# Attention outputs: reciprocals of the softmax sums spread by GpSimd's DMAs through DRAM, outputs multiplied and split by GpSimd, low part of q by VectorE

## The chip, the cores and the metric

The kernel runs on one core of one Trainium2 chip. The metric is the device time of one execution in microseconds, as a median of three runs. The core has five engines, each working through its own list of instructions in order: PE (TensorE, with its weight loads shown apart as PEld), DVE (VectorE), ACT (ScalarE), POOL (GpSimd) and SP (SyncE, which issues most DMAs). Some DMAs are issued from POOL.

## The reference

One layer of a diffusion backbone over 1024 latent tokens and 256 context tokens, in fp32. What matters here is the attention between the two feed-forward halves, and that its output is projected afterwards.

```python
def gqa_attend(q, k, v):
    s = jnp.einsum('btkgd,blkd->bkgtl', q, k, preferred_element_type=jnp.float32) * (HEAD_DIM ** -0.5)
    p = jax.nn.softmax(s, axis=-1).astype(v.dtype)
    return jnp.einsum('bkgtl,blkd->btkgd', p, v)
...
        x = x + 0.5 * ml[2] * swiglu(modulate(rms_norm(x, norm1_g[layer]), ml[0], ml[1]),
                                      ffn1_w_in[layer], ffn1_w_out[layer])
...
        o_l = latent_attention(q_l, k_all, v_all)

        x = x + ml[5] * merge_branches(y_conv_l, o_l, gt_l, w_branch_conv[layer],
                                       w_branch_attn[layer], w_out[layer])
...
        x = x + 0.5 * ml[8] * swiglu(modulate(rms_norm(x, norm3_g[layer]), ml[6], ml[7]),
                                      ffn2_w_in[layer], ffn2_w_out[layer])
    return rms_norm(x, final_g)
```

There are 8 query heads on 2 key heads, each 128 wide; 1024 latent queries look at 1280 keys.

## The kernel before

**Precision.** Every fp32 product is three matmuls (`mm3`): each operand is split into a high part, rounded to the fast matmul type, and a low part, what is left; high by high, high by low and low by high are added up in PSUM. A split is therefore two instructions: a copy that rounds (on ACT, a CAST in the profile) and a subtraction (on DVE unless told otherwise).

**Attention.** The work is cut into 16 units: 8 heads, each with the queries 0 to 511 (`C0`) and 512 to 1023 (`C1`). Unit 0 is head 0 with `C0`, unit 15 is head 7 with `C1`. A unit goes through these steps:
- `begin`: q of the unit is split into the two `qs` tiles of 128x512; the high part by ACT, the low part by POOL.
- `scores`, four times, for 128 queries each: matmuls against the context keys (`kc`) and twice 512 latent keys (`kl`); DVE finds the maxima (`m`, `nm`), ACT takes the exponentials (`pc`, `pl`) and sums each row on the way, DVE adds the sums (`rsum`).
- `turn`, ten times, one for each 128 keys: PE transposes four 128x128 blocks into a PSUM bank (`pt`), and the bank is split into `pts`, high part by ACT, low part by DVE. There are two such banks.
- `values`, ten times: three matmuls of `pts` with the values add up in the one PSUM bank `po`. Turns run three steps ahead of values (`AHEAD = 3`).
- `output`: four rows of sums become reciprocals (`rinv`, 128 queries on the partitions by 4), PE transposes each, spread over 128 columns, into a `pt` bank, so that each partition holds the 512 reciprocals; ACT copies `po` to the head's tile `q` of 128x1024, and DVE multiplies the copy by the bank.

**What runs beside it.** The loop over `units[1:]` writes the scores of a unit between the turns and values of the unit before it. Up to unit 12 or so it also has `fillers`: matmuls of the convolution branch, which give PE something else to do. They run out at about 1740 us, and what follows, from there to about 1867 us, is called the tail here: scores of the last units, turns and values, and after the last scores turns and values alone. At the end of the tail come the merges (projections of the head outputs), which need all heads' outputs in split form: `split_output` makes `oh` and `ol` of 128x1024 for each head. From unit 13 on the loop writes the splits of heads 0 to 5 between the steps; head 6 follows, then head 7 in two halves of 512.

**Order.** The kernel is written in the Tile framework; a scheduler settles each engine's order when the program is built, so instructions move ahead of the place where they are written if their operands allow it. In this way parts of the later stage `late_steps` come into the tail: tiles of 128x512 of the modulation weights are loaded (`rawm`, by SP), and DVE adds them up (`macc`).

**Tiles that are shared.** `ttile` hands out 11 buffers of 128x512: `qs`, `rawm`, and the loads `ga` and `z` of the merges take turns in them. SP issues loads in order, so a load that waits for a buffer holds back the loads behind it. The heads' outputs and the `pl` and `pc` tiles are among 38 buffers of 128x1024. All instructions go through the helper `Engine.issue`, so the profile calls all of them line 90; they are told apart by their tiles.

Of the kernel before, what the change touches and what calls it, by code (L numbers as in the profile page):

```python
# [9 lines left out]
F32 = mybir.dt.float32  # L10
# [8 lines left out]
P = 128  # L19
# [7 lines left out]
NQ = 8  # L27
# [8 lines left out]
C0, C1, CC = ("l", 0, 512), ("l", 512, 512), ("c", 0, CT)  # L36
# [15 lines left out]
def tile_dit_layer(  # L52
# [44 lines left out]
    act, dve, pool, pe, sp = (Engine(e) for e in (nc.scalar, nc.vector, nc.gpsimd, nc.tensor, nc.sync))  # L97
# [7 lines left out]
    dram = ctx.enter_context(tc.tile_pool(name="dram", bufs=1, space=DRAM))  # L105
# [3 lines left out]
    def uniq(s):  # L109
        n_tiles[0] += 1  # L110
        return f"{s}_{n_tiles[0]}"

    def atile(name, shape=(P, SLOT), dt=F32):
        return apool.tile(list(shape), dt, tag="A", name=uniq(name))

    def ttile(name, n=512, dt=F32):
        t = tpool.tile([P, 512], dt, tag="t", name=uniq(name))
        return t[:, :n]

    def small(name, n, dt=F32):  # L120
        return spool.tile([P, n], dt, tag=f"s{n}_{name}", name=uniq(name))
# [4 lines left out]
    def ps_t(n=512):  # L126
        return psum.tile([P, 512], F32, tag="t", name=uniq("pt"), bufs=2)[:, :n]
# [4 lines left out]
    def matmul(out, w, x, start, stop, pinned=False, on=False):  # L132

        inst = pe.matmul(out, w, x, start=start, stop=stop, skip_group_check=on)
        if pinned:
            tc.keep_in_program_order(inst)

    def transpose(out, in_, pinned=False):
        n = in_.shape[0]
        inst = pe.transpose(out, in_, ident[:n, :n])  # L140
        if pinned:
            tc.keep_in_program_order(inst)
# [43 lines left out]
    def col(name, k=0):  # L186
        o = voff[name] + k
        return cols[:, o : o + 1]
# [8 lines left out]
    def split(src, hi, lo, lo_eng=None, hi_eng=None):  # L197

        if hi_eng is dve:
            dve.tensor_copy(out=hi, in_=src)  # L200
        else:
            act.copy(out=hi, in_=src)
        (lo_eng or dve).tensor_sub(out=lo, in0=src, in1=hi.bitcast(F32))
# [257 lines left out]
    def run(steps, n=None):  # L461

        if n is None:
            for _ in steps:
                pass
        else:
            for _ in range(n):
                next(steps, None)
# [597 lines left out]
    for k in range(4):  # L1066
        if k % 2:
            half1.shifted(h0[k][:, 0], k, xh[k])
        else:
            dve.tensor_scalar(  # L1070
                out=h0[k][:, 0], in0=xh[k], scalar1=gain1["l"][:, k : k + 1], scalar2=modl[:, k : k + 1],
# [43 lines left out]
    hd = dram.tile([NH, P, L], F32, name="hd")  # L1115
# [85 lines left out]
    for j in range(NH):  # L1201
        half1.side = side(j) if j >= SIDE_FROM else None
        u, c = half1.next_first()
        v, b = half1.second(u)
# [25 lines left out]
    for d in range(0, KD, 2):  # L1230
        t = ttile("cx")
# [7 lines left out]
        for e in range(2):  # L1239
            te = t[:, e * CT : (e + 1) * CT]  # L1240
            dve.scalar_tensor_tensor(
                out=te, in0=pt[:, e * CT : (e + 1) * CT], scalar=gate1["c"][:, d + e : d + e + 1], in1=te, op0=ALU.mult, op1=ALU.add
# [71 lines left out]
    for i in range(KD):  # L1314
        u = atile("u")
# [5 lines left out]
        for ch, bg, gc in mixed():  # L1321
            gate(gcd, i, ch, gc)
            o = ch[1]
            y = ttile("y")
            dve.tensor_scalar(out=y, in0=u[:, o : o + 512], scalar1=col("w1", i), scalar2=None, op0=ALU.mult)
            for j in (0, 2):
                a, b = max(o, 1 - j), min(o + 512, L + 1 - j)
                ya = y[:, a - o : b - o]
                dve.scalar_tensor_tensor(
                    out=ya, in0=u[:, a + j - 1 : b + j - 1], scalar=col(f"w{j}", i), in1=ya, op0=ALU.mult, op1=ALU.add  # L1330
# [42 lines left out]
    for kt in range(10):  # L1373
        ch = CC if kt < 2 else C0 if kt < 6 else C1
        o = (kt if kt < 2 else (kt - 2) % 4) * P
# [67 lines left out]
    q_f = []  # L1443
# [65 lines left out]

    o_parts = [None] * NQ  # L1510

    def split_output(hd, *chunks):
        if o_parts[hd] is None:
            o_parts[hd] = atile("oh", dt=F32R), atile("ol", dt=F32R)
        a, b = chunks[0][1], chunks[-1][1] + 512
        split(q_f[hd][:, a:b], *(t[:, a:b] for t in o_parts[hd]))

    class Unit:
        def __init__(self, hd, ch):
# [2 lines left out]
        def begin(self):  # L1522
            o = self.ch[1]
            self.qs = [ttile("qs", dt=F32R) for _ in range(2)]
            split(q_f[self.hd][:, o : o + 512], *self.qs, pool)
            self.pc = atile("pc", (P, 4, CT))
            self.pl = []
            self.rsum = small("rsum", 4)
# [37 lines left out]
        def values(self, kt, pts):  # L1566
# [5 lines left out]
            matmul(po, vh, pts[:, 1], start=False, stop=False)  # L1572
            matmul(po, vl, pts[:, 0], start=False, stop=(kt == 9))

        def output(self):
            rinv = small("rinv", 4)
            of = q_f[self.hd][:, self.ch[1] : self.ch[1] + 512]
            dve.reciprocal(out=rinv[:], in_=self.rsum[:])
            pr = ps_t()
            for qt in range(4):  # L1580
                transpose(pr[:, qt * P : (qt + 1) * P], rinv[:, qt : qt + 1].to_broadcast([P, P]))
            act.copy(out=of, in_=self.po)
            dve.tensor_mul(out=of, in0=of, in1=pr)

    def seconds():

        turned = []

        def value():
            u, kt, pts = turned.pop(0)  # L1590
            u.values(kt, pts)
            if kt == 9:
                u.output()

        for u in units:
            for kt in range(10):
                turned.append((u, kt, u.turn(kt)))
                if len(turned) > AHEAD:
                    value()
                yield  # L1600
        while turned:
            value()
            yield
# [4 lines left out]
    def merge(j, ch):  # L1608

        if j not in m_hi:  # L1610
            m_hi[j], m_lo[j] = atile("mh", dt=F32R), atile("ml", dt=F32R)
        if j not in wa:
            wa[j] = load_cols(w_ba[0], j * P)
        w, o = wa[j], ch[1]
        ga, z = ttile("ga"), ttile("z")
        sp.dma_start(out=ga, in_=gad[j, :, o : o + 512])
        sp.dma_start(out=z, in_=zd[j, :, o : o + 512])
        ps = ps_s()
        terms = [
            (w[0][:, k], w[1][:, k], *(t[:, o : o + 512] for t in o_parts[k])) for k in range(KD)  # L1620
        ]
        for k in range(KD - 1):
            mm3(ps, terms, k, k + 1)
            yield
        mm3(ps, terms, KD - 1)
        dve.tensor_mul(out=ga, in0=ga, in1=ps)
        dve.tensor_add(out=ga, in0=ga, in1=z)
        split(ga, m_hi[j][:, o : o + 512], m_lo[j][:, o : o + 512])
        yield

    units = [Unit(hd, ch) for hd in range(NQ) for ch in (C0, C1)]
    u = units[0]
# [26 lines left out]
    for n_unit, u in enumerate(units[1:], 1):  # L1659
        u.begin()  # L1660
        for n in (3, 2, 3, 2):
            u.scores(len(u.pl))
            for _ in range(n):
                run(rest, 1)
                if len(u.pl) < 4:
                    run(fill, 1)
            if n == 2:
                run(fill, 1)
            if n == 2 and n_unit >= 13:
                split_output(next(to_split), C0, C1)  # L1670
    run(fill)
    run(rest, 4)
    split_output(NQ - 2, C0, C1)
    split_output(NQ - 1, C0)
    merges = (step for j in range(2) for step in merge(j, C0))
    for _ in rest:
        run(merges, 2)
    run(merges)
    split_output(NQ - 1, C1)


    for j in range(KD):
# [7 lines left out]
    for ch in (C0, C1):  # L1690
        o = ch[1]
        for d in range(KD):
# [7 lines left out]
                out=xs(d, ch), in0=ps, scalar=modl[:, 40 + d : 41 + d], in1=xs(d, ch), op0=ALU.mult, op1=ALU.add  # L1700
# [16 lines left out]
        out=gf[:], in0=cols[:, voff["gf"] : voff["gf"] + 8], scalar1=math.sqrt(D), scalar2=None, op0=ALU.mult  # L1717
# [46 lines left out]
    for j in range(NH):  # L1764
        if j > 1:
            run(last_steps, 3)
        u, c = fast.next_first()
        v, b = fast.second(u)
# [81 lines left out]
```

## Time and profile before

| | us |
|---|---|
| median of three runs | 2693.46 (2692.87 to 2695.69) |
| the profiled execution, its own time | 2692.97 |
| its span, from the first to the last instruction | 2691.1 |
| PE busy in the span | 2646.4 |
| DVE busy | 2016.0 |
| ACT busy | 1178.8 |
| POOL busy | 513.8 |
| attention: copy of the first unit's output, of the last | 1516.34, 1866.86 |

An engine's busy time is summed over its instructions, with overlaps counted once. Idle time of an engine costs something only where another waits for it. The views used below are: the page; the instructions of one tile; busy time in stretches of the span; the timeline of one engine; and the chain of waits, which goes back from the last instruction of a stretch to whatever released each piece of work. In the chain a row has its start, its length, the engine and the tile (or the DMA) that it stands for.

### The profile page before, as it was taken

The numbers are of one execution on the slowest core, as the hardware profiler recorded it, in microseconds if no ns is written. First come the engines' busy times: TensorE is split into PE (matmuls) and PEld (weight loads), VectorE is DVE, ScalarE is ACT, GpSimd is POOL, SyncE is SP. The second block draws the span as 40 slices with busy tenths as digits, with TensorE's granted clock in tenths as the row PEclk, the third lists the DMA queues.
The fourth block names the chain that finished last, engine by engine and source line by source line (L and its number), as shares of the span: only waits on it lengthen the run. The fifth ranks groups of instructions, "written<-read, shape, count | busy, mean of one in ns | idle before, by whom it ended". The sixth has DMA issues, their size and how long they took to land.

```text
span 2691.1 us, 36996 instructions
## 1 busy us (share of the span) xinstructions
PE 2646.4 (98%) x13437; PEld 2228.1 (83%) x13437; DVE 2016.0 (75%) x3363; ACT 1178.8 (44%) x2324; POOL 513.8 (19%) x403
## 2 busy tenths in 40 slices
PE   8999999999999999999999999999999999999998
PEld 5787899888778878888999888877888788888888
DVE  5788966888887899877487666785658886667885
ACT  6523454433454633333245666664236333334453
POOL 0144201221010044333023111000001442321200
PEclk9999999999999999999999999999999999999999
DMA  8565465346974345332213311011733552327841
GB/s 317 196 204 176 146 215 173 117 126 215 286 179 122 111 155 180 108 111 94 80 48 105 112 48 44 28 52 59 246 119 129 180 168 87 95 86 278 192 91 63
DMA packets 368206, 372.68 MB, mean 138 GB/s; under 512 B 18822, under 2 KB 257560, under 8 KB 368024
## 3 DMA queue, kind: packets, MB, share of 16 engines
q1 hardware_dynamic: 359000, 353.03, 39.9%
q0 software_dynamic: 9024, 17.30, 4.0%
q8 instruction: 105, 1.72, 0.3%
q14 instruction: 77, 0.63, 0.1%
HBM read 302.59 MB, written 67.63 MB: 138 GB/s over the span
## 4 chain that ended last, share of the span: by engine, by line
PE 91%; DVE 4%; DMA 2%; issue 2%; ACT 1%; POOL 0%; SPq 0%; DVEq 0%; POOLq 0%; ACTq 0%
PE ps L90 75%; PE pt L90 8%; PE po L90 7%; DMA rawm<-in_w_mod_dram 1%; DVE r L90 1%; DVE macc L90 0%; DMA ws<-in_ffn_w_out_dram 0%; DVE wl L90 0%; DVE nt L90 0%; DMA raw<-in_ffn_w_in_dram 0%; POOL s L90 0%; DVE uc L90 0%; DVE y L90 0%; DVE m L90 0%; DVE ol L90 0%
## 5 line engine op out<-in xcount | busy, mean ns | idle before, releaser
L90 PE MATMUL ps<-r,wl 128*128 128x512 f32 x5196 | 1206.5, 391 | 10.3 <-DVE wl L90 4.2
L90 PEld LDWEIGHTS ps<-r,wl 128*128 128x128 f32 x5196 | 974.1, 189 | 219.3 <-DVE wl L90 6.3
L90 ACT CAST wl<-s 128x512 fp32r<-128x512 f32 x254 | 156.7, 619 | 321.2 <-PE ps L90 218.7
L90 POOL TENSOR_TENSOR s<-raw 128x512 f32<-128x512 f32 x64 | 94.4, 1474 | 1051.2 <-DMA raw<-in_ffn_w_in_dram 630.7
L90 ACT CAST wl<-raw 128x512 fp32r<-128x512 f32 x287 | 177.5, 619 | 215.3 <-PE ps L90 153.9
L90 DVE TENSOR_TENSOR wl<-raw,wl 128x512 fp32r<-128x512 f32 x287 | 201.9, 705 | 62.1 <-ACT wl L90 60.3
L90 DVE TENSOR_TENSOR wl<-s,wl 128x512 fp32r<-128x512 f32 x254 | 230.4, 908 | 19.9 <-ACT wl L90 18.5
L90 POOL TENSOR_TENSOR s<-raw,s 128x512 f32<-128x512 f32 x64 | 103.8, 1623 | 361.1 <-DVE wl L90 361.1
L90 DVE SCALAR_TENSOR_TENSOR macc<-rawm,silu_c,macc 128x512 f32<-128x512 f32 x178 | 148.7, 852 | 25.0 <-DMA rawm<-in_w_mod_dram 24.3
L90 PE MATMUL ps<-wh,r 128*128 128x256 f32 x768 | 141.6, 285 | 0.0
L90 DVE TENSOR_TENSOR pts<-pt,pts 128x512 fp32r<-128x512 f32 x160 | 108.6, 686 | 41.4 <-ACT pts L90 40.2
L90 DVE TENSOR_TENSOR u<-u,ps 128x512 f32<-128x512 f32 x174 | 118.0, 678 | 27.8 <-PE ps L90 27.7
L90 ACT CAST pts<-pt 128x512 fp32r<-128x512 f32 x160 | 92.8, 592 | 89.5 <-PE pt L90 87.9
L90 DVE TENSOR_REDUCE m<-ps 128x1 f32<-128x512 f32 (+1 forms) x192 | 110.9, 595 | 26.0 <-PE ps L90 24.9
L90 ACT CAST rh<-hid 128x512 fp32r<-128x512 f32 x132 | 81.2, 620 | 107.1 <-PE ps L90 90.4
L90 PE MATMUL ps<-rh,wl 128*128 128x512 f32 x360 | 122.4, 390 | 2.8 <-ACT rh L90 2.8
L90 PEld LDWEIGHTS ps<-wh,r 128*128 128x128 f32 x768 | 120.6, 192 | 0.0
L90 PE MATMUL po<-pts,vh 128*128 128x512 f32 x256 | 111.7, 443 | 1.5 <-ACT pts L90 1.4
L90 PE MATMUL ps<-wl,r 128*128 128x256 f32 x384 | 108.8, 283 | 0.0
L90 PE MATMUL ps<-kl,qs 128*128 128x512 f32 x384 | 106.2, 397 | 0.4 <-ACT pc L90 0.4
L90 DVE TENSOR_TENSOR rl<-hid,rh 128x512 fp32r<-128x512 f32 x132 | 89.9, 684 | 21.7 <-PE ps L90 12.0
L90 ACT CAST wh<-raw 128x512 fp32r<-128x512 f32 (+1 forms) x85 | 67.9, 801 | 84.1 <-PE ps L90 57.7
(312 smaller groups left out, 5100.7 us busy)
## 6 DMA issues: line engine op xcount, KB each, us to landing
raw<-in_ffn_w_in_dram SPq DMA_DIRECT2D x130, 512.0 KB
raw<-in_ffn_w_out_dram SPq DMA_DIRECT2D x72, 512.0 KB
rawm<-in_w_mod_dram SPq DMA_DIRECT2D x136, 256.0 KB
raw<-in_w_in_dram SPq DMA_DIRECT2D x61, 512.0 KB
hid<-hd SPq DMA_DIRECT2D x40, 512.0 KB
ws<-in_ffn_w_out_dram POOLq DMA_DIRECT2D x30, 512.0 KB, 6.5
ucd<-uc SPq DMA_DIRECT2D x25, 512.0 KB
hd<-c SPq DMA_DIRECT2D x40, 256.0 KB
```

The lines of the kernel that those rows point to most:

```text
L90: inst = getattr(self.engine, name)(*args, **kw)
```

## The change

`output` loses the transposes. Instead, a new method `inverse`, written after the fifth `values` step of a unit, takes the reciprocals and issues two DMAs from POOL: the first writes the 128x4 reciprocals to a row of 512 numbers in DRAM, in the order of the queries (each element of 4 bytes goes to a place of its own); the second reads that row back to each of the 128 partitions, into a `ttile` called `rrow`. `output` is then ACT's copy of `po` and a multiplication by POOL. The splits of heads 0 to 6 go from ACT and DVE to POOL, both instructions; the two halves of head 7 (`late=True`) stay with ACT and DVE. The low part of `qs` goes from POOL to DVE.

```diff
-    def split_output(hd, *chunks):
+    def split_output(hd, *chunks, late=False):
         if o_parts[hd] is None:
             o_parts[hd] = atile("oh", dt=F32R), atile("ol", dt=F32R)
         a, b = chunks[0][1], chunks[-1][1] + 512
-        split(q_f[hd][:, a:b], *(t[:, a:b] for t in o_parts[hd]))
+        hi, lo = (t[:, a:b] for t in o_parts[hd])
+        if late:
+            split(q_f[hd][:, a:b], hi, lo)
+        else:
+            pool.tensor_copy(out=hi, in_=q_f[hd][:, a:b])
+            pool.tensor_sub(out=lo, in0=q_f[hd][:, a:b], in1=hi.bitcast(F32))
...
-            split(q_f[self.hd][:, o : o + 512], *self.qs, pool)
+            split(q_f[self.hd][:, o : o + 512], *self.qs)
...
+        def inverse(self):
+            rinv = small("rinv", 4)
+            dve.reciprocal(out=rinv[:], in_=self.rsum[:])
+            row = dram.tile([512], F32, name=uniq("rinvd"))
+            pool.dma_start(out=row.rearrange("(j p) -> p j", p=P), in_=rinv[:])
+            self.rows = ttile("rrow")
+            pool.dma_start(out=self.rows, in_=row.partition_broadcast(P))
+
         def output(self):
-            rinv = small("rinv", 4)
             of = q_f[self.hd][:, self.ch[1] : self.ch[1] + 512]
-            dve.reciprocal(out=rinv[:], in_=self.rsum[:])
-            pr = ps_t()
-            for qt in range(4):
-                transpose(pr[:, qt * P : (qt + 1) * P], rinv[:, qt : qt + 1].to_broadcast([P, P]))
             act.copy(out=of, in_=self.po)
-            dve.tensor_mul(out=of, in0=of, in1=pr)
+            pool.tensor_mul(out=of, in0=of, in1=self.rows)
...
             u.values(kt, pts)
+            if kt == 4:
+                u.inverse()
             if kt == 9:
                 u.output()
...
     split_output(NQ - 2, C0, C1)
-    split_output(NQ - 1, C0)
+    split_output(NQ - 1, C0, late=True)
...
-    split_output(NQ - 1, C1)
+    split_output(NQ - 1, C1, late=True)
```

The scheduler settles the order anew. Three places matter below. The first is PE where unit 12 ends and the values of unit 13 (`po_17316` before, `po_17303` after) begin; `rinv_17276` are unit 12's reciprocals, `vc` and `vh` parts of the values. Before:

```order
L90 MATMUL po_17316<-pts_17248,vc_11566 128x512 x3
L90 MATMUL po_17316<-pts_17259,vc_11566 128x512
L90 MATMUL pt_17278<-ident,rinv_17276 128x128 x4
L90 MATMUL po_17316<-pts_17259,vc_11566 128x512 x2
L90 MATMUL po_17316<-pts_17270,vh_11562 128x512
```

and with the change:

```order
L90 MATMUL po_17303<-pts_17242,vc_11566 128x512 x3
L90 MATMUL po_17303<-pts_17253,vc_11566 128x512
L90 MATMUL ps_17549<-kc_11851,qs_17434 128x256 x2
L90 MATMUL ps_17549<-kc_11851,qs_17435 128x256
L90 MATMUL pt_17295<-ident,pl_16994 128x128
L90 MATMUL pt_17295<-ident,pl_17052 128x128
L90 MATMUL pt_17295<-ident,pl_17103 128x128
L90 MATMUL pt_17295<-ident,pl_17165 128x128
L90 MATMUL po_17303<-pts_17253,vc_11566 128x512 x2
L90 MATMUL po_17303<-pts_17264,vh_11562 128x512
```

The four transposes of reciprocals, which took one of the two `pt` banks, are gone; a turn and three of unit 15's score matmuls stand there.

The second is DVE where the first sums of the modulation weights (`macc`) stand. Before, they follow the last row sum and reciprocal, unit 15's, in the stretch of its last scores:

```order
L90 SCALAR_TENSOR_TENSOR macc_3284_17932<-rawm_17978,silu_c,macc_3284_17932 128x512
L90 SCALAR_TENSOR_TENSOR macc_3284_17932<-rawm_17981,silu_c,macc_3284_17932 128x512
L90 TENSOR_REDUCE rsum_17446<-rs_17625 128x1
L90 RECIPROCAL rinv_17888<-rsum_17446 128x4
L90 SCALAR_TENSOR_TENSOR macc_3284_17932<-rawm_17984,silu_c,macc_3284_17932 128x512
L90 TENSOR_TENSOR pts_17136<-pt_17131,pts_17136 128x512
L90 TENSOR_TENSOR pts_17147<-pt_17142,pts_17147 128x512
L90 SCALAR_TENSOR_TENSOR macc_3284_17932<-rawm_17987,silu_c,macc_3284_17932 128x512
L90 TENSOR_TENSOR pts_17158<-pt_17153,pts_17158 128x512
```

With the change they begin later, among the turns of unit 14:

```order
L90 TENSOR_SCALAR macc_3300_17916<-rawm_17917,silu_c 128x512
L90 TENSOR_TENSOR pts_17491<-pt_17486,pts_17491 128x512
L90 TENSOR_TENSOR pts_17527<-pt_17522,pts_17527 128x512
L90 SCALAR_TENSOR_TENSOR macc_3300_17916<-rawm_17920,silu_c,macc_3300_17916 128x512
L90 TENSOR_TENSOR pts_17539<-pt_17534,pts_17539 128x512
L90 SCALAR_TENSOR_TENSOR macc_3300_17916<-rawm_17923,silu_c,macc_3300_17916 128x512
L90 TENSOR_TENSOR pts_17578<-pt_17573,pts_17578 128x512
L90 SCALAR_TENSOR_TENSOR macc_3300_17916<-rawm_17926,silu_c,macc_3300_17916 128x512
L90 TENSOR_TENSOR pts_17589<-pt_17584,pts_17589 128x512
```

The sums have moved past the last scores, and two or three of the turns' subtractions stand between them; `rawm_17923` lies in the buffer that `rrow_17383`, unit 13's, had.

The third is POOL, which before had nothing between its last `qs` and the work of the second feed-forward half. With the change this stands there (`rrow_17156` is unit 12's row, `rrow_17383` unit 13's, `rrow_17610` unit 14's, `rrow_17795` unit 15's; `q_13261` is head 6, `q_13262` head 7):

```order
L90 CAST oh_17545<-q_12921 128x1024
L90 TENSOR_TENSOR q_13261<-q_13261,rrow_17156 128x512
L90 TENSOR_TENSOR ol_17546<-q_12921,oh_17545 128x1024
L90 CAST oh_17657<-q_12922 128x1024
L90 DMA rinvd_17793<-rinv_17791 128x4x1
L90 TENSOR_TENSOR ol_17658<-q_12922,oh_17657 128x1024
L90 DMA rrow_17795<-rinvd_17793 128x512
L90 TENSOR_TENSOR q_13261<-q_13261,rrow_17383 128x512
L90 CAST oh_17708<-q_13261 128x1024
L90 TENSOR_TENSOR ol_17709<-q_13261,oh_17708 128x1024
L90 TENSOR_TENSOR q_13262<-q_13262,rrow_17610 128x512
L90 TENSOR_TENSOR q_13262<-q_13262,rrow_17795 128x512
```

Products of units 12 to 15, splits of heads 4 to 6 and unit 15's two DMAs share one queue, in this order.

## The prediction

> **What bounds the kernel now.** I read the page first, then busy time by stretches around the attention, then the chain of waits in the attention's tail, then single tiles for durations. From the page:
>
> ```profile
> span 2691.1 us, 36996 instructions
> PE 2646.4 (98%) x13437; PEld 2228.1 (83%) x13437; DVE 2016.0 (75%) x3363; ACT 1178.8 (44%) x2324; POOL 513.8 (19%) x403
> ```
>
> ```profile
> PE 91%; DVE 4%; DMA 2%; issue 2%; ACT 1%; POOL 0%; SPq 0%; DVEq 0%; POOLq 0%; ACTq 0%
> ```
>
> PE is busy for 98% of the span and makes 91% of the chain. POOL has 0% of the chain: it is the engine with room. So the change can gain in two ways only: by PE work that goes away, and by stalls of PE that go away. Where the stalls are is seen in busy time by stretches (columns: stretch, its length, then each engine's busy time with instructions, the granted PE clock, DMA share, GB/s):
>
> ```profile
> 1490.00:1740.00 250.00, 248.90 (x1364) 209.07 (x1363) 167.37 (x367) 160.83 (x410) 35.54 (x20) 1.00 0.17 55
> 1740.00:1860.00 120.00, 112.57 (x622) 91.20 (x621) 88.84 (x163) 73.48 (x164) 0.00 (x0) 0.97 0.15 45
> ...
> 1790.00:1815.00 25.00, 21.25 (x106) 16.54 (x105) 18.11 (x34) 14.93 (x34) 0.00 (x0) 0.86 0.21 63
> ...
> 1776.00:1790.00 14.00, 12.98 (x78) 10.70 (x77) 13.00 (x29) 10.14 (x26) 0.00 (x0) 1.00 0.31 95
> 1795.00:1805.00 10.00, 6.52 (x37) 4.70 (x35) 7.64 (x16) 6.22 (x15) 0.00 (x0) 0.90 0.39 113
> 1826.00:1833.00 7.00, 5.76 (x34) 4.49 (x34) 4.22 (x7) 3.10 (x5) 0.00 (x0) 1.00 0.00 0
> ```
>
> While the convolution's matmuls fill in (1490 to 1740), PE is idle for 1.1 of 250 us: there every matmul removed is time saved, and no stall can be. In the tail it is idle for 7.4 of 120 us, and in the 25 us from 1790 its granted clock is 0.86, which makes 21.25 us of matmuls some 0.14 x 21.25 = 3.0 us longer than at full clock. DVE is busy for 13.0 of the 14 us from 1776. What PE waits for there is in the chain of waits of the tail, at two places:
>
> ```profile
> 1796.52 2.76 DMA rawm<-in_w_mod_dram
> 1799.30 0.76 DVE macc L90
> 1800.08 2.68 DMA rawm<-in_w_mod_dram
> 1802.78 0.75 DVE macc L90
> 1803.54 0.61 DVE pts L90
> ...
> 1804.19 1.12 PE pt L90 x4
> ```
>
> ```profile
> 1827.73 0.70 DVE q L90
> 1828.45 1.06 ACT oh L90
> 1829.53 1.22 DVE ol L90
> 1830.75 0.61 DVE pts L90
> ...
> 1831.41 0.66 PE pt L90 x4
> ```
>
> At the first, a sum for a later stage stands in DVE's queue and waits for its load; the subtraction `pts` stands behind it, and PE's next transposes wait for the bank that `pts` would free. At the second, the product, the split of head 6 on ACT and DVE, and again a `pts` behind them.
>
> **The change part by part.** First the transposes of the reciprocals. Their group and what four transposes take in the chain when PE runs undisturbed:
>
> ```profile
> L90 PE MATMUL pt<-ident,rinv x64: 270/272/275, 1518.2 to 1856.5; 128*128 128x128 f32 x64
> ```
>
> ```profile
> 1818.74 0.44 PE pt L90 x4
> 1819.17 0.70 PE po L90 x3
> 1819.88 0.44 PE pt L90 x4
> ```
>
> 272 ns is the modelled length of one, overlapping the next; four advance the chain by 0.44 us. 64 of them are 16 x 0.44 = **7.0 us of PE** gone. Units 0 to 8 end before 1740, so 9 x 0.44 = 4.0 us lie where PE is never idle and are safe; the other 3.1 us lie in the tail, 94% busy, and I count them whole. A turn's bank is also held 16 times less often.
>
> Second, what leaves and joins the other engines, by these rows:
>
> ```profile
> L90 POOL TENSOR_TENSOR qs<-q,qs x16: 1282/1290/2072, 1456.3 to 1709.9; 128x512 fp32r<-128x512 f32 x16
> L90 DVE TENSOR_TENSOR q<-q,pt x16: 676/686/689, 1518.9 to 1867.7; 128x512 f32<-128x512 f32 x16
> L90 ACT CAST oh<-q x9: 614/1047/1072, 1755.3 to 1869.3; 128x1024 fp32r<-128x1024 f32 x7, 128x512 fp32r<-128x512 f32 x2
> L90 DVE TENSOR_TENSOR ol<-q,oh x9: 685/1215/1227, 1756.5 to 1870.2; 128x1024 fp32r<-128x1024 f32 x7, 128x512 fp32r<-128x512 f32 x2
> ```
>
> ```profile
> L90 POOL TENSOR_TENSOR wc<-raw,wc 128x1024 fp32r<-128x1024 f32 x9 | 21.6, 2395 | 110.0 <-ACT wc L90 110.0
> ```
>
> DVE loses 16 products (16 x 0.69 = 11.0) and 7 subtractions (7 x 1.22 = 8.5), and gains 16 subtractions for q's low part, which I take at the same 0.69 (11.0): 8.5 us less, all in the tail. ACT loses 7 x 1.05 = 7.3 us there. POOL gets 16 products at 1.29, 7 subtractions at 2.40, 7 roundings of 128x1024, which no row shows: between 1.2 (half of the two-operand 2.40) and 2.40, I take 1.8; and 32 DMAs. Of those the nearest rows are POOL's own loads for issuing, and for landing the transfer that spreads one row over 128 partitions, from SP's issue at 2304.9 to the DVE instruction that waits for it:
>
> ```profile
> L90 POOL DMA_DIRECT2D ws<-in_ffn_w_out_dram x36: 1199/1222/1444, 701.1 to 2582.6; - x36
> DMA to landing us min/median/max: 5.7/6.5/10.9
> ```
>
> ```profile
> L90 SPq DMA_DIRECT2D mcol<-mrow x1: 476/476/476, 2304.9 to 2304.9; - x1
> ...
> 2307.80 1.10 DVE L90 TENSOR_TENSOR modl<-mcol,bcol 128x4 f32<-128x4 f32 x1 [1.80 <-DMA mcol<-mrow]
> ```
>
> A DMA takes 1.2 us to issue on POOL, up to 2.4 if 512 elements of 4 bytes cost double; it lands after between 2.9 us (2 KB, as here) and 10.9 us (up to 512 KB). I take 1.2 and 2.9, since the sizes are those of `mcol`. POOL waits in its queue for the first landing before it issues the second DMA, and products and splits queue behind that.
>
> Does POOL keep up? The copies of `po`, after which a product can start, come at
>
> ```profile
> 1812.57 0.59 ACT q L90
> ...
> 1825.41 0.59 ACT q L90
> ...
> 1839.45 0.59 ACT q L90
> ```
>
> for units 12, 13 and 14: 12.8 and 14.0 us apart, and over 20 us apart for the units before. Between the products of units 12 and 13 POOL has, by its order, a subtraction, a rounding, a DMA, a subtraction (which covers all but 0.5 us of the landing), a DMA and the product: 2.4 + 1.8 + 1.2 + 2.4 + 0.5 + 1.2 + 1.3 = 10.8 of 12.8 us. It keeps up, by 2 us; with 2.4 for the rounding and both DMAs it is 13.8 and falls behind by 1 us.
>
> Third, the stalls. What goes: the wait for `rawm` at 1796 to 1804, 3.5 us of idle PE (10 less 6.52), and the slow clock after it, 3.0; head 6's split, 0.9 (7 less 5.76, of which 0.3, the wait for the copy of `po`, stays); and from 1776 to 1790, where the same sums and splits crowd DVE, 0.8 of 1.0. Together 8.2 us.
>
> What comes in their place: (a) the sums stand among unit 14's turns now, and `rawm_17923` needs the buffer of unit 13's row. That is free when POOL's product ends: copy 1825.41 + 0.59, product 1.29, 0.4 for SP's issue, landing 2.7 as in the chain: 1830.4. DVE comes to that sum some 1.5 to 2 us after the copy, at about 1827.5, and waits 2.9 us. PE meanwhile has the values of turns made ahead and a second bank, about 1.6 us: 1.3 us of idle PE. (b) POOL late by 0 to 4 us, I take 1.0. (c) In unit 15 ACT rounds head 7's first half behind a product of 1.29 in place of 0.69, with `pts` behind it: 0.5, of 0 to 1. (d) The clock: a gap remains, though shorter, so I keep half of the loss, 1.5 of 0 to 3.0. Together 4.3 us. The dozen other POOL instructions (`wc` low parts) then queue behind DMAs' waits, with a unit's time, 20 us and more, of slack: nothing. Unit 15's own product is followed by the merges, for which PE has work of other heads: nothing; without that cover it is 0.6 us. The DMAs move 256 KB a unit on 16 DMA engines used to 15%: nothing.
>
> The sum: 2692.97 (the profiled execution's own time, span and 1.9 us around it) - 7.0 - 8.2 + 4.3 = **2682.1, say 2682 us**. The median of the runs is 0.5 us higher than that execution, which I leave within the error. Best case, nothing in place of the stalls: 2678, and 2675 if the other 2 us of idle time in the tail go too. Worst case, with only the safe 4.0, (a) at the landing's full 2.7, (b) 4, (c) 1 and (d) 3.0: -4.0 - 8.2 + 10.7 = -1.5, 2691. Its own range is 2675 to 2691.
>
> **The rivals.** *The tail gives everything back.* PE saves 4.0 us up to 1740, and in the tail each wait removed shows up as another: 2689. For it: DVE there is busy for 13.0 of 14 us, and `rawm` loads wait for buffers that POOL frees. Against it: of the stall at 1796, 5.4 us of the 7.7 shown are loads, and loads that start earlier land earlier; and splits that leave DVE and ACT stand in no way any more.
>
> *POOL becomes the bound of the tail, slower.* One mechanism: POOL's time between products exceeds the 12.8 us between units, unit 13's product comes late, then `rawm_17923`, then DVE's sum, the `pts` behind it, and PE. Its price, by the slow ends of the rows: POOL's subtractions and products 1.6 times as long (the slowest `qs` took 2072 against 1290 ns): 3.8 each for subtraction and rounding, 2.1 for a product, DMAs 2.4, landing 10.9. Between units 12 and 13: 3.8 + 3.8 + 2.4 + 10.9 + 2.4 + 2.1 = 25.4 us, 12.6 late, and about 5 more from the units before, of which nothing is made up: 18 us of idle PE on top of 2682, 2700. It decides from 12.8 us on, and the kernel is slower once POOL is some 17 us late. For it: writes of 4 bytes are in no row of this case. Against it: `mcol`'s 2.9 us, and a slow `qs` is the exception (median 1290).
> By the Trainium skill, page "DMA: Bandwidth & Descriptors", section "Rules for kernel authors", a transfer whose last dimension isn't contiguous is lowered to one descriptor per element; that would be 512 here, and its "Specifications" table says that writes under 512 bytes are read, modified and written. No run here shows such a transfer. The rule raises the chance of this rival, not its price.
>
> *POOL slows DVE.* DVE's subtraction has two speeds already, by what else goes on:
>
> ```profile
> L90 DVE TENSOR_TENSOR wl<-raw,wl 128x512 fp32r<-128x512 f32 x287 | 201.9, 705 | 62.1 <-ACT wl L90 60.3
> L90 DVE TENSOR_TENSOR wl<-s,wl 128x512 fp32r<-128x512 f32 x254 | 230.4, 908 | 19.9 <-ACT wl L90 18.5
> ```
>
> The second, whose operand POOL makes, takes 0.2 us more. If the `pts` of units 12 to 15 did so, 40 x 0.2 = 8 us of DVE, about half of it behind PE's own 1.14 us a step: 2682 + 4 = 2686. Against it: `pts` reads PSUM, and its 160 instructions took 658/690/694 ns in a stretch where POOL worked for 35 of 250 us.
>
> ```profile
> L90 DVE TENSOR_TENSOR pts<-pt,pts x160: 658/690/694, 1490.5 to 1857.3; 128x512 fp32r<-128x512 f32 x160
> ```
>
> The Trainium skill, page "GPSIMD Engine Reference", section "Specifications", has GpSimd's way to SBUF shared with VectorE, with contention for instructions with two SBUF inputs; the `wl` rows agree, and `pts` has one.
>
> **How the numbers follow.** This kernel's runs tell a change from none at about 0.2%, 5.4 us: faster is below 2688.1, slower above 2698.8. Forecast 0.58 (0.53 faster, 0.05 within); the tail gives back 0.17 (0.05 faster, 0.12 within); POOL the bound 0.14 (0.12 slower, 0.02 within); POOL slows DVE 0.11 (0.08 faster, 0.03 within). Faster 0.66, within 0.22, slower 0.12. The range for 8 in 10 reaches from the best case, 2675, past the forecast's worst and the first rival to 2695, which leaves out most of the second rival.
>
> **What would show it.** No `rinv` transposes, and PE's work up to the end of the fill shorter by 4 us. POOL's products starting within 1 us of the end of ACT's copy in units 11 to 14; the DMA's issue at 1.2 us and the row's landing under 4 us, or else the second rival. The chain of the tail without `ol` and with a wait for `rawm` of under 3 us in unit 14; clock above 0.9 there. `pts` at 690 ns, or the third. It would be wrong if the merges or the second feed-forward half began later than 7 us ahead of now, because sums that were put off late hold up DVE there.

## The result, and the profile after

| | median of the runs, us | ratio to before, 95% interval |
|---|---|---|
| before | 2695.38 (2692.87 to 2698.09, 6 runs) | |
| with the change | 2683.95 (2682.67 to 2685.79, 6 runs) | 0.9959 [0.9947, 0.9972] |

The change is faster by 0.41%, 11.0 us of 2695.38, and between 0.28% and 0.53%: clear of the 0.2% that can be told apart. The profiled execution of the changed kernel took 2685.79 us, the slowest of the six, with a span of 2684.0 us; it came to the attention 1.8 us later than the execution profiled before, with nothing changed up to there. So the two traces are best compared over the attention alone, from the first to the last of ACT's sixteen copies of `po`. Busy time by stretches (columns as before: stretch, length, busy time of PE, PEld, DVE, ACT and POOL, granted clock, DMA share, GB/s), of the kernel before:

```profile
1516.34:1866.86 350.52, 341.98 (x1872) 283.82 (x1871) 239.13 (x491) 217.09 (x531) 29.45 (x17) 0.99 0.15 49
```

and with the change, with two shorter stretches:

```profile
1518.04:1859.13 341.09, 335.03 (x1817) 278.65 (x1815) 229.26 (x483) 212.80 (x533) 79.36 (x65) 0.99 0.26 63
1795.00:1805.00 10.00, 9.81 (x56) 7.72 (x54) 6.46 (x16) 9.22 (x26) 6.26 (x5) 1.00 0.29 79
1815.00:1840.00 25.00, 20.53 (x102) 15.94 (x101) 14.12 (x20) 9.91 (x17) 6.43 (x5) 0.86 0.32 86
```

The attention is 9.4 us shorter. PE's busy time fell by 341.98 - 335.03 = 6.95 us, its idle time from 8.54 to 6.06 us, by 2.5. The stretch from 1795, where PE had been idle for 3.5 of 10 us, is full; the matmuls that stood there now run some 14 us earlier (unit 12's copy ends at 1799.03, before at 1813.15), and PE is not idle there either: it is busy for 20.0 of the 20 us from 1775. But a new hole stands at 1815 to 1840: 4.5 us idle, and the granted clock of 0.86 has moved there. The hole on PE's and on DVE's timeline (the bracket is the idle time before the row, and who ended it):

```profile
1817.47 0.40 PE L90 MATMUL po<-pts,vh 128*128 128x512 f32 x1
1821.51 1.11 PE L90 MATMUL pt<-ident,pl 128*128 128x128 f32 x4 [3.64 <-DVE pts L90]
```

```profile
1813.35 0.48 DVE L90 TENSOR_SCALAR macc<-rawm,silu_c 128x512 f32<-128x512 f32 x1
...
1819.43 1.42 DVE L90 SCALAR_TENSOR_TENSOR macc<-rawm,silu_c,macc 128x512 f32<-128x512 f32 x1 [3.19 <-DMA rawm<-in_w_mod_dram]
1820.78 0.68 DVE L90 TENSOR_TENSOR pts<-pt,pts 128x512 fp32r<-128x512 f32 x1
```

The old stall in a new place: a sum waits for its load, `pts` stands behind it, PE's transposes behind `pts`; and the four transposes after the hole are shown at 1.11 us where 0.66 is usual, which is the slow clock. POOL at that time:

```profile
1805.35 0.78 POOL L90 DMA_DIRECT2D rinvd<-rinv  x1 [1.61 <-DVE rinv L90]
1806.15 2.41 POOL L90 TENSOR_TENSOR ol<-q,oh 128x1024 fp32r<-128x1024 f32 x1
1814.88 0.58 POOL L90 DMA_DIRECT2D rrow<-rinvd  x1 [6.32 <-DMA rinvd<-rinv]
1815.48 1.30 POOL L90 TENSOR_TENSOR q<-q,rrow 128x512 f32<-128x512 f32 x1
```

The write of unit 15's reciprocals is issued at 1805.35; after the subtraction behind it POOL stands for 6.3 us, until 1814.88, for its landing. Unit 13's product, which needs nothing from it, queues behind and starts at 1815.48. ACT's copy had ended at 1813.19:

```profile
1812.60 0.59 ACT L90 COPY q<-po 128x512 f32<-128x512 f32 x1
```

So the product is 2.3 us late. In the 16 units the products of 0 to 2, 10, 11 and 13 start over 1 us after the copy (7.2 us in unit 0, 4.8 in unit 10). The instructions on the reciprocals show that every unit's write lands as late as this one:

```profile
L90 POOL DMA_DIRECT2D rinvd<-rinv x16: 764/787/830, 1489.2 to 1805.4; - x16
DMA to landing us min/median/max: 8.7/8.8/9.2
```

### The profile page after: what moved, and what is told of

Same layout as the page of the kernel before. It is cut to its first block, busy times and chain, and to the rows that moved or that the text cites. A ratio compares the mean times of both kernels' runs of the same rounds, so it can differ in the third digit from the quotient of the medians.

```text
span 2684.0 us, 36956 instructions
## 1 busy us (share of the span) xinstructions
PE 2639.7 (98%) x13373; PEld 2221.6 (83%) x13373; DVE 2006.2 (75%) x3356; ACT 1171.3 (44%) x2317; POOL 557.9 (21%) x449
## 4 chain that ended last, share of the span: by engine, by line
PE 84%; DVE 4%; DMA 2%; issue 2%; POOL 1%; ACT 1%; SPq 0%; DVEq 0%; POOLq 0%; ACTq 0%
PE ps L90 69%; PE pt L90 7%; PE po L90 7%; DVE wl L90 1%; DMA raw<-in_ffn_w_in_dram 1%; DMA ws<-in_ffn_w_out_dram 1%; DVE r L90 1%; DMA rawm<-in_w_mod_dram 1%; POOL s L90 0%; DVE macc L90 0%; POOL ol L90 0%; DVE u L90 0%; DVE uc L90 0%; DVE nt L90 0%; DVE v L90 0%
```

## The experiments

Each ran beside the kernel before on the same chip. "Stretch" is the time from the first to the last copy of `po` in the profiled execution, "PE" its busy time there; without them the row is 350.52 and 341.98 for the kernel before.

| run | median, us | before, us | ratio, 95% interval | stretch | PE |
|---|---|---|---|---|---|
| the change, again (e5) | 2686.10 | 2696.20 | 0.9961 [0.9948, 0.9973] | 339.03 | 333.51 |
| splits alone (e3) | 2690.71 | 2696.22 | 0.9980 [0.9971, 0.9988] | 345.81 | 339.69 |
| all but the splits (e4) | 2689.90 | 2696.22 | 0.9977 [0.9966, 0.9987] | 346.41 | 337.85 |
| the change, q's low part on POOL (e8) | 2684.32 | 2696.20 | 0.9962 [0.9948, 0.9975] | 343.54 | 335.64 |
| the change, pieces of 16 bytes (e1) | 2687.30 | 2696.22 | 0.9964 [0.9951, 0.9976] | 337.30 | 332.47 |
| the change, sums held back (e2) | 2678.58 | 2696.22 | 0.9932 [0.9920, 0.9944] | 332.55 | 330.81 |
| the same, again (e9) | 2676.82 | 2695.34 | 0.9932 [0.9920, 0.9945] | 332.47 | 330.71 |
| held, pieces of 16 bytes (e10) | 2679.67 | 2695.34 | 0.9945 [0.9932, 0.9957] | 332.66 | 330.75 |
| before, sums held back (e6) | 2693.01 | 2696.20 | 0.9987 [0.9978, 0.9996] | 345.99 | 339.61 |
| splits alone, sums held back (e7) | 2688.11 | 2696.20 | 0.9973 [0.9961, 0.9984] | 341.28 | 338.02 |
| the change, each row written twice (e11) | 2726.30 | 2695.34 | 1.0120 [1.0105, 1.0136] | 380.65 | 340.69 |

**Which half of the change makes the gain?** One kernel has only the splits of heads 0 to 6 on POOL, the other everything but them.

```diff
# splits alone: the kernel before, with
+            pool.tensor_copy(out=hi, in_=q_f[hd][:, a:b])
+            pool.tensor_sub(out=lo, in0=q_f[hd][:, a:b], in1=hi.bitcast(F32))
# all but the splits: the change, with
-        if late:
+        if True:
             split(q_f[hd][:, a:b], hi, lo)
```

> The kernel before, with only the splits of heads 0 to 6 moved to POOL; reciprocals, products and q's low part as before. Theory (7.0 us of the gain are PE's transposes, the rest is the tail): the transposes stay, the stall of 3.5 us with its slow clock at the sums stays in some form, since sums still stand ahead of the last reciprocal; head 6's split and the crowd on DVE go: 1 to 4 us under before, 2691 to 2694 where before is 2695. Rival (the splits make the gain): 2684 to 2687.

> The change, with the splits of heads 0 to 6 back on ACT and DVE; reciprocals by GpSimd's DMAs, products on POOL, q's low part on DVE. Theory: the 7.0 us of PE are there, and POOL, without the splits, is on time for unit 13 but for the 9 us of the landing; the splits' stalls stay: 2695.4 - 7.0 +- 2 = 2686 to 2690. Rival (the splits make the gain): 2692 to 2696.

The splits alone take 5.5 us off their own before, somewhat more than the 1 to 4 expected, and all but the splits 6.3 us, at the slow edge of what was expected. The two add up to 11.8, and the change takes 11.0: both halves count, about equally, each with 2 to 3 us to either side. In the second, PE's idle time between the copies is as long as before (346.41 - 337.85 = 8.6). Head splits stand in its chain of waits again (`ol` at 1788.57 and 1796.93), and one wait of 3.2 us is behind a sum that waits for its load. Its busy time falls by 4.1 us and not by 7, in part since a slow clock makes matmuls longer: it is 0.93 from 1790 and 0.86 from 1815, each for 25 us, where before has one such stretch of 0.86. That is 0.07 x 22.41 = 1.6 us more; the other 1.3 us are within what busy time differs by between kernels with the same matmuls (339.61 and 338.02 us in e6 and e7, both at clock 1.00).

**Is the slow landing a matter of the pieces?** The row is written in another order, so that each partition writes its four numbers as one piece of 16 bytes; the product reads the row through a view.

```diff
-            pool.dma_start(out=row.rearrange("(j p) -> p j", p=P), in_=rinv[:])
+            pool.dma_start(out=row.rearrange("(p j) -> p j", p=P), in_=rinv[:])
...
-            pool.tensor_mul(out=of, in0=of, in1=self.rows)
+            o3 = of.rearrange("d (j p) -> d j p", j=4)
+            pool.tensor_mul(out=o3, in0=o3, in1=self.rows.rearrange("d (p j) -> d j p", j=4))
```

> The change, with the reciprocals written to DRAM as 128 pieces of 16 bytes (element p*4+j) in place of 512 of 4, and POOL's product reading the row through a view that undoes that order; the instructions stand in the same order on every engine. Theory (the many small writes are what is slow: 8.8 us to land in the changed kernel): landing 3 to 4 us, POOL no longer blocked for 9 us a unit, unit 13's product starts within 0.2 us of the end of ACT's copy (2.3 us late before), the row of unit 15 is read before unit 13 ends and doesn't meet the load of rawm; PE's idle 3.6 us in unit 14's first turns shrinks to under 1.5 and the clock stays near 1.0: 2678 to 2681 us. Rival (a write to DRAM through GpSimd's queue takes 9 us whatever its pieces): landing 8 to 9 us, 2683 to 2685. Rival (the stall comes from the sums' place in DVE's order alone): landing short, stall still 3 us or more, 2683 to 2685.

The instructions on the reciprocals, and POOL at unit 13's product, in this run:

```profile
L90 POOL DMA_DIRECT2D rinvd<-rinv x16: 543/572/628, 1489.3 to 1807.2; - x16
DMA to landing us min/median/max: 1.7/1.7/5.3
```

```profile
1807.82 2.40 POOL L90 TENSOR_TENSOR ol<-q,oh 128x1024 fp32r<-128x1024 f32 x1
1810.16 0.57 POOL L90 DMA_DIRECT2D rrow<-rinvd  x1
1815.21 1.54 POOL L90 TENSOR_TENSOR q<-q,rrow 128x512 f32<-128x512 f32 x1 [4.49 <-ACT q L90]
```

1.7 us in place of 8.8: it is the pieces, by their number, their size or their order in DRAM, which this run changes together. POOL now waits for ACT's copy and not for the landing. PE's longest wait in unit 14's turns falls to 1.4 us, with a clock of 1.00 from 1815 to 1840; on DVE the second sum has its data 2.8 us after the end of the first (1817.03), where that took 5.6 us with the change:

```profile
1821.61 0.66 PE L90 MATMUL pt<-ident,pl 128*128 128x128 f32 x4 [1.43 <-DVE pts L90]
```

```profile
1815.28 1.75 DVE L90 TENSOR_SCALAR macc<-rawm,silu_c 128x512 f32<-128x512 f32 x1
...
1819.80 1.15 DVE L90 SCALAR_TENSOR_TENSOR macc<-rawm,silu_c,macc 128x512 f32<-128x512 f32 x1 [1.57 <-DMA rawm<-in_w_mod_dram]
```

So the theory holds for the links that the trace shows, and the stretch is 1.7 to 3.8 us shorter than in the two executions of the changed kernel. The medians don't show it: 0.9964 against 0.9959 and 0.9961, intervals of 0.25% each, and a product that takes 1.55 in place of 1.29 us by its strided reading. 2678 to 2681 had been expected, and 2687.30 was measured, so the forecast of the time missed, and so did those of the rivals, 2683 to 2685. Whether a gain of some 2 us is there is left open. The rest of the stall stays, as the second rival had it: PE is idle for 2.9 of the 25 us from 1815, where the change has 4.5, since the sum stands where it stood.

**Are the sums the stall?** The first sum is kept behind what is written before it on DVE, so all of them come after the attention.

```diff
-                        dve.tensor_scalar(out=acc, in0=raw, scalar1=s, scalar2=None, op0=ALU.mult)
+                        first = dve.tensor_scalar(out=acc, in0=raw, scalar1=s, scalar2=None, op0=ALU.mult)
+                        if m == 6 and half == 0:
+                            tc.keep_in_program_order(first)
```

> The change, with the first sum of the modulation weights (macc) kept behind what is written before it on DVE, so that all sums stand after unit 15's split, among the merges. Theory (the stall of 3.6 us in unit 14's first turns is DVE's wait for rawm, and the slow clock follows from it): PE idle there under 0.5 us, clock 1.0 from 1815 to 1840, the 0.6 us in unit 15 gone too: 2684 - 3.6 - 3.0 - 0.6 = 2677 us. Rival (POOL's late product holds the tail by another way, through head 7's split or the turns): stall stays, 2683 to 2685. Rival (the sums are needed early: put off, they hold up the second feed-forward half): tail shorter, but what follows the attention longer by as much, 2682 to 2690.

Expected 2677, measured 2678.58, and 0.9932 of before, 0.27% under the change. The stretches of this run:

```profile
1519.94:1852.49 332.55, 330.81 (x1815) 276.61 (x1813) 224.13 (x475) 212.05 (x532) 79.36 (x65) 1.00 0.23 55
...
1815.00:1840.00 25.00, 24.76 (x140) 20.29 (x141) 13.57 (x21) 11.42 (x20) 6.60 (x5) 1.00 0.14 32
```

PE is idle for 1.7 of 333 us and the clock is full; nothing is paid back later, since from the last copy to the end of the span it takes 824.2 us, as before. POOL's product of unit 13 is still 2.4 us late here (1817.24, the copy ends at 1814.86), so that lateness by itself costs PE next to nothing. The same edit in the kernel before, and in the one with the splits alone:

> The kernel before, with only the first sum of the modulation weights kept behind what is written before it on DVE, so that the sums stand among the merges. Theory (of the tail's stalls before, the largest, 3.5 us of idle PE and 3.0 us of slow clock from 1795 on, came from sums that waited for their loads): clock 1.0 throughout the tail, 5 to 8 us under before, 2688 to 2691 where before is 2696. Rival (the crowd on DVE and the splits stall PE all the same): within 3 us of before, 2693 to 2696.

> The kernel before, with the splits of heads 0 to 6 on POOL and the sums held back; the reciprocals are still transposed by PE and the products still made by DVE. It differs from the changed kernel with held sums (0.9932 of before) by the reciprocals, the products and q's low part alone, in a tail without stalls. Theory (those are worth the 64 transposes, 16 x 0.44 us on PE, and nothing else): 7.0 +- 1.0 us slower than that kernel, 2685 to 2687 where before is 2696. Rival (the transposes cost less, since PE takes them while it would wait): 2679 to 2682.

In the kernel before it brings 3.2 us (the interval is 1.1 to 5.9), less than the theory's 5 to 8, and 2693.01 lies in the range of the rival: the clock is 1.00 throughout, but PE is idle for 350.52 - 341.98 = 8.5 us before and still for 6.4 with it, because the splits still stand in the chain of waits of the tail (three of its rows):

```profile
1802.17 1.06 ACT oh L90
...
1807.63 1.13 DVE ol L90
1808.77 0.61 DVE pts L90
```

The theory was right on the clock and wrong on the price, which the rival had; the stalls of the tail cover for one another. With the sums held and the splits on POOL, the kernel with transposes has 338.02 us of PE against 330.81 with the spread by DMAs: 7.2 us, the transposes' 7.0 within the error. 2685 to 2687 had been expected, and 2688.11 was measured. The medians are further apart than the busy times, 0.9973 against 0.9932, which is 11 us of 2696 with some 4.5 us to either side; 1.5 us of that is idle time (3.26 against 1.74), and the rest, 2.3 us, is within the error.

**Does POOL's lateness cost anything else?** First both edits together, then the opposite: each row of reciprocals written twice, the second copy spread, the first unread.

```diff
-            row = dram.tile([512], F32, name=uniq("rinvd"))
-            pool.dma_start(out=row.rearrange("(j p) -> p j", p=P), in_=rinv[:])
+            for _ in range(2):
+                row = dram.tile([512], F32, name=uniq("rinvd"))
+                pool.dma_start(out=row.rearrange("(j p) -> p j", p=P), in_=rinv[:])
```

> The change with held sums once more, as the one to compare the next with on one chip: 0.993 of before.

> The change with held sums and with the reciprocals written as 128 pieces of 16 bytes. Theory (the landing of 9 us costs PE time only through rawm, whose loads wait for buffers that POOL's late products free): without early sums nothing is left to gain, since PE is idle for only 1.7 of 333 us between the first and the last copy of po; within 2 us of the run with held sums alone. Rival (POOL's lateness also holds PE through other buffers): 3 us or more below it.

> The change with each unit's reciprocals written twice, to two rows in DRAM, the second of which is spread; the first is left unread. Theory (writes of 4 bytes are worked off one after another, and POOL's wait for the landing is what makes the products late): the second write lands 17 to 18 us after its issue, POOL is blocked for some 17 us a unit, the product of unit 13 is 8 us or more later than in the changed kernel, and the stall in unit 14's turns grows by about as much: 2690 to 2696 where the changed kernel has 2685. Rival (two writes go side by side): landing 9 to 11 us, 2683 to 2688.

With the sums held back a fast landing brings nothing: 0.9945 against 0.9932, the stretch 332.66 against 332.47. It is even slower by 2.9 us, where at most 2 us of difference had been expected, and each of its five times lies above each of the five of e9. The stretches don't show where the 2.9 us go: the two executions that were profiled, the slowest of e9 and the fastest of e10, differ by 0.9 us only. POOL's 9 us a unit are then free. In the change without held sums, waiting for twice as long is not free: 1.0120 of before, 42 us over the change, where 5 to 11 had been expected. POOL in the tail of that run:

```profile
1839.09 0.78 POOL L90 DMA_DIRECT2D rinvd<-rinv  x1
1847.68 0.77 POOL L90 DMA_DIRECT2D rinvd<-rinv  x1 [7.81 <-issue]
1848.46 1.27 POOL L90 TENSOR_TENSOR q<-q,rrow 128x512 f32<-128x512 f32 x1
1849.69 2.34 POOL L90 TENSOR_TENSOR ol<-q,oh 128x1024 fp32r<-128x1024 f32 x1
1856.88 0.59 POOL L90 DMA_DIRECT2D rrow<-rinvd  x1 [4.85 <-DMA rinvd<-rinv]
```

The second write is issued 8.6 us after the first, though it waits for no other engine ("issue" is a wait that the profile can't put down to anyone), and POOL then waits again for the landing: 17.8 us in this unit and 17 to 21 in the 16 units, as expected in sum but not in the way expected. Two long waits of PE come of it, of 15.0 and of 12.4 us, with clocks of 0.59 and 0.73 in the 25 us from 1840 and from 1790. The waits by engine:

```profile
PEld pt L90 <- DVE pts L90: 21.9, 7, 15.4
...
ACT pl L90 <- POOL ol L90: 13.6, 1, 13.6
DVE macc L90 <- POOL q L90: 13.4, 1, 13.4
PEld ps L90 <- ACT pl L90: 12.6, 1, 12.6
```

One goes by the known way: the first sum waits for POOL's product of unit 12, which starts 20.8 us after its copy (1848.46 and 1827.63), and `pts` stands behind the sum. The other is new: unit 14's exponentials `pl` go to buffers that POOL's splits free, so ACT waits for POOL, and PE's scores for ACT.

**Did q's low part have to leave POOL?**

```diff
-            split(q_f[self.hd][:, o : o + 512], *self.qs)
+            split(q_f[self.hd][:, o : o + 512], *self.qs, pool)
```

> The change, with the low part of q left on POOL as before. On POOL it then stands behind the second DMA of a unit in most units, which waits some 9 us for the first one's landing. Theory (POOL's block of 9 us a unit hurts whatever stands behind it and is wanted soon): q's low part comes late, PE's scores wait in most of 15 units for some us each, 2690 to 2760. Rival (scores have enough slack): 2683 to 2687.

0.9962 against 0.9961 for the change beside it: no difference. The theory fell, and the rival holds: although these subtractions stand behind the second DMA of most units, the scores have the slack. (The stretch of the one profiled execution is 343.54, 2.5 to 4.5 us longer than the change's; the medians don't bear that out.)

> The changed kernel itself, as the one to compare the others of this call with on one chip. 0.996 of before, 2685 where before is 2696.

This second set of runs of the changed kernel came out as the first, 0.9961 and 0.9959. Its trace differs in the hole: PE waits 3.1 us in unit 14 and not 3.6, and the slow clock is shorter, 0.93 over the 25 us from 1815:

```profile
1815.00:1840.00 25.00, 21.04 (x108) 16.38 (x107) 14.80 (x21) 9.39 (x16) 5.01 (x4) 0.93 0.39 110
```

## Why the prediction was right

2682 was forecast, 2684 measured, and the sum of 10.9 us under the profiled execution before stands against 11.0 by the ratio, whose interval is 7.5 to 14.3. So near a hit is luck in part: the transposes were priced right and the stalls of before went, but POOL did not keep up, the load that is waited for is another than the forecast had, and what comes in place of the stalls was put too small, by up to 2.8 us. By its steps:

- **Transposes, 7.0 us of PE.** Right: 7.2 by the pair of kernels without sums in the tail. The two traces of before and after give 6.95, and 8.5 with the second execution (e5), whose clock was slow for less time.
- **What goes of the stalls, 8.2 us.** Right for the places: 1795 to 1805 is full at clock 1.00, and head 6's split has left the chain. What each was worth alone can't be read off, since holding the sums back brings 3.2 us in the kernel before and 7.3 (0.9959 less 0.9932) in the changed one, though the two are not clear of each other's error.
- **What comes in their place, 4.3 us.** Too small. (a) A wait for `rawm` in unit 14's turns was forecast at 1.3 us of PE and is 3.6 (3.1 in e5). That a sum waits, `pts` behind it and PE behind `pts`, was right. The reason given for it, `rawm_17923` waiting for POOL's late product, was not. The sum that waits is the second, one before `rawm_17923`. Its load was issued at 1813.85, just after the first sum had ended (1813.83), and its data came at 1819.43, 5.6 us on, while a load took 2.7 us in the chain before. (One or two subtractions stand between the sums, as the order shows, not two or three.) Why the load was slow stays open. The read of unit 15's row, issued at 1814.88, falls into that time, and with that read well before (e1) the load takes 2.7 us. But in the kernel without the splits on POOL (e4) the same sum waits as long, though unit 13's product starts 0.1 us after its copy. There the load is issued at 1811.22, and the read of the row only at 1816.01:

```profile
1816.01 0.56 POOL L90 DMA_DIRECT2D rrow<-rinvd  x1 [10.33 <-DMA rinvd<-rinv]
...
1817.27 0.75 DVE L90 SCALAR_TENSOR_TENSOR macc<-rawm,silu_c,macc 128x512 f32<-128x512 f32 x1 [3.38 <-DMA rawm<-in_w_mod_dram]
...
1818.68 1.12 PE L90 MATMUL pt<-ident,pc 128*128 128x128 f32 x4 [3.17 <-DVE pts L90]
```

The view of DMA of e4 from 1811.2 to 1817 (each digit is 0.145 us) shows the load alone, standing still for some 1.7 us, and no packet of the read:

```profile
DMA  0000002163320000000000004022366916266310
...
q1 hardware_dynamic: 144, 0.26, 20.8%
```

So neither the read nor POOL's late product makes that wait. A write in pieces of 4 bytes was under way there until 1815.47; whether such writes hold up loads, no run tries alone. (b) 1.0 us was kept for POOL's lateness. It is 2.3 us late, and with the sums held (e2) just as late, where PE is idle for 1.7 us in all: it costs about nothing. (c), 0.5 us in unit 15, is 0.6, but as another wait for `rawm`. (d) Half of the clock's loss, 1.5 us, was kept. In the first trace all of it is there, 0.86 over 25 us, 0.14 x 20.53 = 2.9 us; in the second (e5) it is half, 0.07 x 21.04 = 1.5.
- **Prices on POOL.** Issues were taken at 1.2 us and are 0.79 and 0.57; the rounding at 1.8 and is 1.04; product and subtraction, 1.29 and 2.40, are right. The landing of the write was taken at 2.9 us from a transfer of the same size, and is 8.8: the term that was mis-sized. The prediction named 4-byte writes as the unknown and had up to 10.9 for them. By the Trainium skill, page "DMA: Bandwidth & Descriptors", section "Rules for kernel authors", such a write is one descriptor per element; 8.8 us for 512 pieces against 1.7 for 128 of the same bytes fits it, and a price by pieces would have been better than a price by bytes.
- **"It keeps up, by 2 us".** It didn't. Between unit 12's product and unit 13's there are 16.4 us, where 10.8 were forecast, and the copies are 14.2 apart (1799.03 and 1813.19). The sum of 10.8 left 0.5 us for the landing beyond what a subtraction covers; the forecast's own bound of 10.9 us for a landing would have left 8.5, and POOL stood for 6.3. Unit 14's copy, 18.6 us after unit 13's, let it catch up.
- **POOL as the bound, slower: 0.14.** Its first step came, since POOL needs more than the 12.8 us from which it was to decide, and its landing is nearer this rival's 10.9 than the forecast's 2.9. The loss didn't come: 2.3 us late is far from the 17 that it was to take. With twice the block it came, at 1.0120: the decision lies between 9 and 18 us of waiting a unit, and the price beyond it is higher than the rival had it, since a second way through ACT's buffers opens.
- **POOL slows DVE: 0.11.** Not for `pts`: 658/690/694 ns before, the same with the change. It does for the sums, below.
- **Its signs.** The landing (8.8 us, under 4 forecast), the products of units 11 and 13 (2.3 us after the copy, under 1 forecast), the wait for `rawm` (3.2 us, under 3) and the clock in the first trace (0.86, above 0.9) came out against it, the last two by little. The missing transposes, `pts` and what follows the attention came out for it: that takes 824.9 us against 824.2, so the sums are not paid for there.

The sum with the give-back of the first trace (3.6 + 0.6 + 2.9 = 7.1 in place of 4.3) would have been 8.1 us under before; the attention is 9.4 shorter there. The last 1.3 us are not assigned, and are less than two executions of the changed kernel differ by (341.09 and 339.03).

## What to carry to other kernels

A detour through DRAM by small DMAs can replace PE work where PE is the bound, but its price here went by how the bytes are cut into pieces and not by the bytes, and the engine that issues the second step stands still for the first one's landing: count what is queued behind it, and write few long pieces. Where a tail loses time to a wait, look for the instruction of a later stage that was moved ahead of the tail's own work; keeping one such sum back brought another 0.27% here, two thirds of what the change brought, and left POOL's delay without a cost. Stalls that cover for one another can't be priced one by one: by the medians, the same edit was worth 3 us before the change and 7 after it.

## What the runs showed of the hardware

- A DMA of 512 pieces of 4 bytes to DRAM lands 8.7 to 9.2 us after its issue on POOL in the changed kernel, one of 128 pieces of 16 bytes after 1.7 (5.3 once in e1), and both move 2 KB. For most of that time the trace shows the DMA engines idle. In the changed kernel's view of DMA from 1805 to 1816 (each digit is a fortieth, 0.28 us) they show work at 1806.7, just after the issue, once more at 1811.4, where instructions are loaded, and then only from 1814.6 on, when the landing is over:

```profile
DMA  0000005000000000000000080000000000005220
...
rinvd<-rinv POOLq DMA_DIRECT2D x1, 2.0 KB, 9.2
```

- POOL stood still before it issued a second such DMA (e11): 8.6 us from one issue to the next with nothing to wait for, and 7.9 to 12.3 in the 16 units. The kernel is built with `dynamic_dma_scratch_size=1024`; whether that setting makes this wait, or the 9 us of the landing, was not tried.
- A sum on DVE takes longer while POOL works on two operands: in the run with pieces of 16 bytes, the first sum starts as POOL's product does (1815.21, 1.54 us) and takes 1.75 us where 0.48 is usual. The second sum, which reads two tiles of SBUF, takes 1.42 us beside POOL's subtraction in the changed kernel and 0.75 in e4, where POOL does nothing. The Trainium skill, page "GPSIMD Engine Reference", section "Specifications", has GpSimd's way to SBUF shared with VectorE, with contention for instructions in a 2-port mode or with two SBUF inputs. The second sum agrees with that, and so does `pts`, which reads one operand from PSUM and didn't slow; in which mode the first sum ran, with one tile as input, no trace shows.
- The granted clock fell after short waits of PE. After 3.6 us it is 0.86 over 25 us, after 3.1 in the same place (e5) 0.93, and after 1.4 (e1) it stays at 1.00. In the kernel before, a wait of 2.0 us soon after one of 1.1 was enough for 0.86.
